# Score rows of 640 keys cut at key 384, and the second halves of the keys loaded from there

## The chip, the cores and the metric

The kernel runs on one core of a Trainium2 chip. The metric is the device time of one execution in microseconds (us). Three runs of the kernel before took 960.04, 960.36 and 960.93 us, so the median is 960.36 us.

## The reference

One layer of a hybrid decoder on 1024 positions of width 1024: a norm and one wide projection, then differential softmax attention (8 heads, two maps each) beside gated linear attention (4 heads), then an output projection and a norm around the residual. The change is in the differential attention. Per head `h`, query block of 128 rows and map `m`:

```python
s = jnp.einsum('bqhmd,bkhmd->bhmqk', qb, k)          # two maps of 64 dims
mask = key_pos[None, :] <= q_pos[:, None]            # causal
p = jax.nn.softmax(jnp.where(mask, s, -jnp.inf), axis=-1)
w = p[:, :, 0] - lam * p[:, :, 1]
out = jnp.einsum('bhqk,bkhv->bqhv', w, v)
```

Everything is computed to float32 accuracy. Each operand is kept as a rounded part `hi` and a remainder `lo`. For the scores the two parts of a map (64 dims each) lie one above the other in 128 partitions: `k` holds (hi, lo), `ks` holds (lo, hi), and two matmuls with the same query tile, `sc<-k,q` and `sc<-ks,q`, give the whole product.

## The kernel before, in words

The program has three stages. The first makes the projections by a fast block scheme (matmuls `x`, `y`, `z`) with the gated attention in between. The second, from about 615 us to 910 us of the profile, runs three streams that `merge` (L1238) lays into one program order by planned times: `all_scores` (L1376), `all_values` (L1480: transposes `wtr`, products `po`, norms `ms`) and `out_early` (L1585: parts of the output projection, `ypart`). The third finishes the output (`yps`). On PE, TensorE's queue, this order is kept as written. On the other engines and on SP, the queue of most loads, a scheduler that simulates a time line may reorder what does not depend on one another.

`all_scores` goes through the heads 0 to 7 and in each through the query blocks 7 down to 0. Block `qb` needs `n = (qb + 1) * 128` keys. `parts_of` (L1270) cuts `n` at 512, since a bank of PSUM holds 512 columns: n = 1024, 896, 768 and 640 make two parts, the smaller ones one. `scores` (L1299) runs one pair of matmuls a part into one of three banks in turn; DVE (VectorE) then adds the mask, stores the part in `p0` or `p1` and takes the row's minimum on the way (L1335; `maskt` is a strip of zeros with the triangle of one block at its end). ACT (ScalarE) makes the exponentials when a row's last part is in, POOL (GpSimd) and DVE weigh and subtract the maps.

Keys and queries lie in DRAM (`qk_d`) and are loaded in two halves of 512 keys by `load_qk` (L1151) through SP: one DMA a map for `q` and `k`, two for `ks`. A tile has a place named by its tag and pool: the second halves of all heads share `k1` and `ks1` in `kp`, the queries `q0` and `q1`; the first halves of even heads are in `k0`, `ks0` of `kp`, those of odd heads in `k0`, `ks0` of `smp`, the pool of stage two. A load into a place waits until PE has read the last tile there. The loads of head h + 1 are written behind query block 4 of head h (L1382 on), together with the second half of head 0's values `v` while h is 0.

`attn_norm` (L1431) of the last head keeps its gate in the places `q1` (first half) and `k1` (second half), which are free by then.

Of the kernel before, what the change touches and what calls it, by code (L numbers as in the profile page):

```python
# [8 lines left out]
F32 = mybir.dt.float32  # L9
F32R = mybir.dt.float32r  # L10
# [4 lines left out]
P = 128  # L15
S = 1024
# [15 lines left out]
def hymba_kernel(  # L32
# [47 lines left out]
    def cols(half):  # L80
        return slice(half * 512, half * 512 + 512)
# [14 lines left out]
    eps_t, mhalf = eps_t[:, :1], eps_t[:, 1:]  # L96
    pool.memset(eps_t, EPS)
    pool.memset(mhalf, -0.5)
    NZ = 512
    maskt = const.tile([P, NZ + P], F32, name="maskt")  # L100
    pool.memset(maskt, 0.0)
    pool.affine_select(
# [40 lines left out]
    def mm(*a, **k):  # L143
        tc.keep_in_program_order(pe.matmul(*a, **k))  # L144
# [32 lines left out]
    kp = ctx.enter_context(tc.tile_pool(name="kp", bufs=1))  # L177
# [969 lines left out]
    def chain(*streams):  # L1147
        for st in streams:
            yield from st

    def load_qk(h, n, half, maps=(0, 1)):  # L1151

        if maps[0]:
            t = qk[h, n, half]
        elif h % 2 and half == 0 and n != "q":
            t = smps[0].tile([P, 2, 512], F32R, tag=f"{n}0", name=f"{n}0")
        else:
            t = kp.tile([P, 2, 512], F32R, tag=f"{n}{half}", name=f"{n}{half}")
        for m in maps:
            d = qk_d["q" if n == "q" else "k"][h][m, :, :, cols(half)]  # L1160
            if n != "ks":
                ins = sp.dma_start(fp(t[:, m]), d.rearrange("t p s -> (t p) s"))
            else:
                for i in range(2):
                    ins = sp.dma_start(fp(t[64 * i : 64 * i + 64, m]), d[1 - i])
        qk_load[:] = [ins.ins]
        qk[h, n, half] = t

    qk, smps, qk_load = {}, [], []
# [97 lines left out]
        if first:  # L1267
            tc.keep_in_program_order(ins)

    def parts_of(n):  # L1270
        return [(0, n)] if n <= 512 else [(0, 512), (512, n)]

    def load_v(h):
        v = [smp.tile([P, NT, P], F32R, tag="v", name=f"v{t}", bufs=4) for t in range(2)]
# [24 lines left out]
    def scores(h, qb):  # L1299

        n = (qb + 1) * P
        qc = slice(qb % 4 * P, qb % 4 * P + P)
        st = const.tile([P, 6], F32, tag="stt", name="stt", bufs=4)
        if h == 0 and qb == NT - 1:
            for row, i in ((4, 7), (5, 6)):
                p1s[row] = pp.tile([P, (i + 1) * P], F32, tag=f"p0_{i}", name="p1", bufs=2)
        p0 = pp.tile([P, n], F32, tag=f"p0_{qb}", name="p0", bufs=1 + (qb > 5))
        if h == 0 and qb < 2:
            p1s[qb] = smp.tile([P, 512], F32, tag=("r", "fold")[qb], name="p1", bufs=1)
        p1 = p1s.pop(qb, None) or smp.tile([P, S], F32, tag="p1", name="p1", bufs=2)  # L1310
        for m, p in enumerate((p0, p1)):
            q = qk[h, "q", qb // 4][:, m, qc]
            parts = parts_of(n)
            if h == DA_HEADS - 1 and (qb, m) in ((1, 1), (0, 0), (0, 1)):

                parts = [(0, 512)]
            for i, (a, b) in enumerate(parts):
                sc = sc_bank("sc", [P, 512])
                for j, name in enumerate(("k", "ks")):
                    for half in range(2):  # L1320
                        lo, hi = max(a, half * 512), min(b, half * 512 + 512)
                        if lo < hi:
                            mm(
                                sc[:, lo - a : hi - a], q,
                                qk[h, name, half][:, m, lo - half * 512 : hi - half * 512],
                                start=(j == 0), stop=(j == 1),
                            )
                e = min(b, n)
                last = i == len(parts) - 1

                forced = (h, qb) == (0, NT - 2) or (h, qb, m) == (0, 3, 0)
                forced = forced or ((h, qb) == (0, 4) and m + i > 0)
                behind = tc.issue_after(lowest[0]) if forced else nullcontext()
                with behind:
                    ins = dve.tensor_tensor_reduce(  # L1335
                        p[:, a:e], sc[:, : e - a],
                        maskt[:, NZ + P - (e - a) :] if last else maskt[:, : e - a],
                        1.0, 3e38 if i == 0 else st[:, 4 + m : 5 + m], ALU.add, ALU.min,
                        st[:, m : m + 1] if last else st[:, 4 + m : 5 + m],
                    )  # L1340
                if (h, qb) == (0, NT - 1):
                    lowest[:] = [ins.ins]
                c = 0.08 + (e - a) / 512 * 0.56
                if last:
                    act.activation(
                        p[:, :n], p[:, :n], AF.Exp, bias=st[:, m : m + 1], scale=-1.0,
                        accum_out=st[:, 2 + m : 3 + m],
                    )
                if last and m:
                    rec = dve.reciprocal(st[:, 4:6], st[:, 2:4])  # L1350
                    if h == 0 and qb in (4, 5):
                        lowest[:] = [rec.ins]
                    pool.tensor_scalar(
                        p1[:, :n], p1[:, :n], st[:, 5:6], lam, ALU.mult, ALU.mult
                    )
                    if qb != 5:
                        while mixed:
                            with tc.issue_after(ins.ins):
                                mixed.pop(0)()

                    def mix_maps():
                        dve.scalar_tensor_tensor(
                            p0[:, :n], p0[:, :n], st[:, 4:5], p1[:, :n], ALU.mult, ALU.subtract
                        )
                        w[h, qb] = p0

                    if h == 0 and qb > 2:
                        mixed.append(mix_maps)
                    else:
                        mix_maps()  # L1370
                    c += 0.25 + n / 1024 * 1.4
                yield c
# [39 lines left out]
        dve.tensor_tensor(lo[:, :n], pt[:, :n], fp(hi[:, :n]), ALU.subtract)  # L1412
        return hi, lo

    turned_last, squared_last = [], []

    def weigh(po, half, kts, v, wt):

# [12 lines left out]
    def attn_norm(h, half, o, po):  # L1431
        if h == DA_HEADS - 1 and not half:
            with tc.issue_after(squared_last[1]):
                act.copy(o, po)
        if h < DA_HEADS - 1:
            gate = smp.tile([P, 512], F32, tag="gate", name="gate", bufs=2)
        else:
            gate = kp.tile([P, 512], F32, tag=("q1", "k1")[half], name="gate")
        with tc.issue_after(qk_load[0]):
            sp.dma_start(gate, g_d[h][:, cols(half)])  # L1440
        sq = smp.tile([P, 512], F32, tag="r", name="sq", bufs=1)


        hl = smp.tile([P, 512], F32R, tag="sq_hl", name="sq_hl", bufs=1)
        fold = smp.tile([P, 512], F32, tag="fold", name="fold", bufs=1)
        act.activation(fold[:64], o[64:], AF.Square)
        ending = h == DA_HEADS - 1 and half
        with tc.issue_after(turned_last[0]) if ending else nullcontext():
            act.activation(sq[:64], o[:64], AF.Square)
        dve.tensor_tensor(sq[:64], sq[:64], fold[:64], ALU.add)  # L1450
        ins = act.copy(hl[:64], sq[:64]).ins
        if ending:
            squared_last.append(ins)
        dve.tensor_tensor(hl[64:], sq[:64], fp(hl[:64]), ALU.subtract)
        if h == DA_HEADS - 1:

            dve.scalar_tensor_tensor(gate, o, sub_g, gate, ALU.mult, ALU.mult)
        for _ in range(4):
            yield 0.0
        n_tr[0] += 1  # L1460
        ms = bank(TR[n_tr[0] % 2], [P, 512], "ms")
        mm(ms, ones, hl, start=True, stop=True)
        if h == DA_HEADS - 1 and not half:
            opened[TR[n_tr[0] % 2]] = None
        r = smp.tile([P, 512], F32, tag="r", name="r", bufs=1)
        act.activation(r, ms, AF.Ln, bias=eps_t, scale=1.0 / P)
        ins = act.activation(r, r, AF.Exp, scale=-0.5).ins
        if ending:
            squared_last.append(ins)
        if h < DA_HEADS - 1:  # L1470
            dve.scalar_tensor_tensor(r, o, sub_g, r, ALU.mult, ALU.mult)
            pool.tensor_tensor(gate, r, gate, ALU.mult)
            sp.dma_start(mixd[h * P : (h + 1) * P, cols(half)], gate)
            stored.append(h)
        else:
            dve.tensor_tensor(gate, gate, r, ALU.mult)
            last_mix[half] = gate
        yield 0.0
# [231 lines left out]
    def last_times(st, dh, part, e):  # L1710
# [8 lines left out]
    T = 8 * 36.0  # L1719
    LAG, SOON = 34.0, 2.0  # L1720
    s_cost = sum(
        2 * sum(0.08 + (min(b, n) - a) / 512 * 0.56 for a, b in parts_of(n)) + 0.25 + n / 1024 * 1.4
        for n in range(P, S + 1, P)
    )
    merge(
# [121 lines left out]
```

## Time and profile before

| what | value |
|---|---|
| median of three runs | 960.36 us |
| the profiled execution | 960.34 us |
| its span, first to last instruction | 958.6 us |
| granted clock of TensorE, mean | 0.998 |
| bytes moved | 220.34 MB |
| loads of keys: `k` 32 of 256 KB, `ks` 64 of 128 KB | 5.5 us and 6.2 us to landing, median |

How to read the lines of the profile: PE is TensorE's matmuls, PEld its weight loads, L144 is the one line through which all matmuls go, so that they are told apart by the names `out<-in` and by shape. A line of a timeline begins with the start in us from the begin of the span and the duration in us. Matmuls are pipelined: the next one starts before the modelled end of the last, so the distance between starts is what one costs. Instructions that only issue a DMA are listed as SPq.

### The profile page before, as it was taken

To read this page: it belongs to the slowest core of one execution; us is meant where nothing else is said; L and a number is where in the kernel's file an instruction comes from. 1 tells how busy PE (TensorE), PEld (TensorE's weight loads), DVE (VectorE), ACT (ScalarE), POOL (GpSimd) and SP (SyncE) were. 2 spreads that over 40 slices of the span, in tenths; PEclk is the share of its full clock that TensorE was granted. 3 is DMA by queue.
4 is the path that set the end of the run, shared out by engine and by line. 5 is a ranking of instruction groups with operands and counts; after the bars stand their busy time and mean duration, and the time that the engine had idled before them with its cause. 6 is when DMAs were issued, how large, how long until landed. Compare 5 with 4: busy or idle time off the path is not lost.

```text
span 958.6 us, 14358 instructions
## 1 busy us (share of the span) xinstructions
PE 948.2 (99%) x4624; PEld 793.2 (83%) x4624; DVE 742.3 (77%) x1476; ACT 604.7 (63%) x1162; POOL 193.9 (20%) x263
## 2 busy tenths in 40 slices
PE   9999999999999999999999999999999999999997
PEld 7877788888888888888888888888888888888885
DVE  5998799996778787687767476588888888898464
ACT  7753355845777556577765444366677677787773
POOL 2001002222141112131100002122222222433321
PEclk9999999999999999999999999999999999999999
DMA  8546367487577897986755498996665679994776
GB/s 285 162 149 172 91 203 244 168 293 249 188 255 242 275 305 255 295 258 216 263 175 154 143 298 265 411 291 217 220 223 193 222 230 349 331 291 105 160 206 141
DMA packets 153258, 220.34 MB, mean 230 GB/s; under 512 B 15776, under 2 KB 85664, under 8 KB 153088
## 3 DMA queue, kind: packets, MB, share of 16 engines
q1 hardware_dynamic: 138736, 177.65, 57.8%
q0 software_dynamic: 14448, 41.79, 14.8%
q8 instruction: 36, 0.59, 0.3%
q14 instruction: 38, 0.31, 0.1%
HBM read 133.93 MB, written 88.60 MB: 232 GB/s over the span
## 4 chain that ended last, share of the span: by engine, by line
PE 96%; DVE 1%; ACT 1%; DMA 1%; issue 0%; POOL 0%; SPq 0%; DVEq 0%; ACTq 0%
PE x L144 23%; PE z L144 16%; PE y L144 16%; PE ypart L144 14%; PE sc L144 7%; PE po L144 5%; PE yps L144 4%; PE wtr L147 3%; PE gpo L144 3%; PE kv L144 1%; PE gkl_ps L144 1%; PE pa L144 1%; PE xT L147 1%; DMA x<-in_x_dram 1%; PE ms L144 0%; PE pk L147 0%
## 5 line engine op out<-in xcount | busy, mean ns | idle before, releaser
L66 ACT CAST w<-w_raw 128x512 fp32r<-128x512 f32 x138 | 85.1, 620 | 70.0 <-PE y L144 31.7
L66 ACT ACTIVATE p<-p,stt 128x896 f32<-128x896 f32 (+7 forms) x128 | 99.3, 777 | 30.8 <-DVE stt L66 29.9
L66 DVE TENSOR_TENSOR w<-w_raw,w 128x512 fp32r<-128x512 f32 x138 | 94.0, 684 | 31.5 <-ACT w L66 31.4
L66 ACT COPY s<-x 128x512 f32<-128x512 f32 x78 | 44.7, 584 | 65.1 <-PE x L144 64.9
L66 DVE CUSTOM_DVE_ANT_0 p<-sc,maskt 128x512 f32<-128x512 f32 (+3 forms) x128 | 74.2, 585 | 14.5 <-PE sc L144 13.2
L66 POOL TENSOR_SCALAR p<-p,stt,lam 128x1024 f32<-128x1024 f32 (+3 forms) x64 | 55.9, 874 | 143.9 <-DVE stt L66 143.8
L144 PE MATMUL z<-s_hi,w 128*128 128x512 f32 x320 | 80.1, 393 | 0.0
L144 PE MATMUL x<-s_hi,w 128*128 128x512 f32 x320 | 80.0, 392 | 0.0
L144 PE MATMUL y<-h_hi,w 128*128 128x512 f32 x320 | 80.0, 392 | 0.0
L144 PE MATMUL ypart<-wo_hi,m_hi 128*128 128x512 f32 x192 | 79.5, 414 | 0.1
L144 PE MATMUL ypart<-wo_hi,m_lo 128*128 128x512 f32 x192 | 75.5, 393 | 0.0
L144 PE MATMUL ypart<-wo_lo,m_hi 128*128 128x512 f32 x192 | 75.4, 393 | 0.0
L66 POOL DMA_DIRECT2D wo_d<-wo_hi x32 | 17.4, 543 | 270.4 <-ACT wo_hi L66 270.4
L144 PEld LDWEIGHTS z<-s_hi,w 128*128 128x128 f32 x320 | 59.8, 188 | 12.3
L144 PEld LDWEIGHTS x<-s_hi,w 128*128 128x128 f32 x320 | 59.7, 188 | 12.3
L144 PEld LDWEIGHTS y<-h_hi,w 128*128 128x128 f32 x320 | 59.7, 188 | 12.2
L144 PE MATMUL sc<-k,q 128*128 128x512 f32 (+1 forms) x192 | 68.9, 362 | 0.1
L144 PE MATMUL sc<-ks,q 128*128 128x512 f32 (+1 forms) x192 | 66.1, 347 | 0.0
L66 ACT CAST wt_hi<-wtr 128x512 fp32r<-128x512 f32 (+1 forms) x80 | 42.8, 534 | 29.0 <-PE wtr L147 28.3
L66 DVE TENSOR_TENSOR wt_lo<-wtr,wt_hi 128x512 fp32r<-128x512 f32 (+1 forms) x80 | 50.6, 633 | 9.9 <-ACT wt_hi L66 9.1
L66 DVE TENSOR_TENSOR w_raw<-w_raw 128x512 f32<-128x512 f32 x80 | 56.2, 703 | 1.4 <-DMA w_raw<-in_w_in_dram 0.4
L66 DVE TENSOR_TENSOR c<-z,s 128x512 f32<-128x512 f32 x48 | 32.8, 687 | 31.3 <-ACT s L66 19.3
(234 smaller groups left out, 2348.0 us busy)
## 6 DMA issues: line engine op xcount, KB each, us to landing
w_raw<-in_w_in_dram SPq DMA_DIRECT2D x40, 512.0 KB, 4.9
wo_d<-wo_hi POOLq DMA_DIRECT2D x32, 256.0 KB, 3.0
q<-q_d SPq DMA_DIRECT2D x32, 256.0 KB, 5.3
k<-k_d SPq DMA_DIRECT2D x32, 256.0 KB, 5.5
ks<-k_d SPq DMA_DIRECT2D x64, 128.0 KB, 6.2
wo_raw<-in_w_out_dram POOLq DMA_DIRECT2D x31, 256.0 KB, 5.0
v<-v_d SPq DMA_DIRECT2D x14, 512.0 KB, 7.7
wo_d<-gqd POOLq DMA_DIRECT2D x22, 256.0 KB, 4.1
```

The source lines that it names most:

```text
L66: ins = op(*a, **k)
L144: tc.keep_in_program_order(pe.matmul(*a, **k))
L147: tc.keep_in_program_order(pe.transpose(dst, src, ident))
```

## The change

From head 1 on a row of 640 keys is cut into 384 and 256 columns instead of 512 and 128. So that no part crosses a border of tiles, the second halves of keys of these heads are loaded from key 384 (`FROM`): tiles of 640 columns, of which rows of 768 keys and more use the part from key 512 on. These wider tiles have one place each in `smp` (`k1`, `ks1`); the first halves of odd heads move into the `k1`, `ks1` of `kp`, which only head 0's second halves had before, and those of even heads stay. The strip of zeros in the mask becomes 384 wide, and the first part of a wide row reads one zero column broadcast. The last head's two gates go into one tile in `q1`.

```diff
-    NZ = 512
+    NZ = 384
...
+    FROM = 384
+
     def load_qk(h, n, half, maps=(0, 1)):
 
         if maps[0]:
             t = qk[h, n, half]
-        elif h % 2 and half == 0 and n != "q":
-            t = smps[0].tile([P, 2, 512], F32R, tag=f"{n}0", name=f"{n}0")
+        elif h and half and n != "q":
+            t = smps[0].tile([P, 2, S - FROM], F32R, tag=f"{n}1", name=f"{n}1")
         else:
-            t = kp.tile([P, 2, 512], F32R, tag=f"{n}{half}", name=f"{n}{half}")
+            other = int(half == 0 and n != "q" and h % 2)
+            t = kp.tile([P, 2, 512], F32R, tag=f"{n}{half + other}", name=f"{n}{half}")
         for m in maps:
-            d = qk_d["q" if n == "q" else "k"][h][m, :, :, cols(half)]
+            cs = slice(FROM, S) if h and half and n != "q" else cols(half)
+            d = qk_d["q" if n == "q" else "k"][h][m, :, :, cs]
...
-    def parts_of(n):
-        return [(0, n)] if n <= 512 else [(0, 512), (512, n)]
+    def parts_of(n, h):
+        if n <= 512:
+            return [(0, n)]
+        cut = FROM if h and n == FROM + 2 * P else 512
+        return [(0, cut), (cut, n)]
...
-                    for half in range(2):
-                        lo, hi = max(a, half * 512), min(b, half * 512 + 512)
-                        if lo < hi:
-                            mm(
-                                sc[:, lo - a : hi - a], q,
-                                qk[h, name, half][:, m, lo - half * 512 : hi - half * 512],
-                                start=(j == 0), stop=(j == 1),
-                            )
+                    at = a if b <= 512 else a - (FROM if h else 512)
+                    mm(
+                        sc[:, : b - a], q, qk[h, name, int(b > 512)][:, m, at : at + b - a],
+                        start=(j == 0), stop=(j == 1),
+                    )
...
-                        maskt[:, NZ + P - (e - a) :] if last else maskt[:, : e - a],
+                        maskt[:, NZ + P - (e - a) :] if last else maskt[:, :1].to_broadcast([P, e - a]),
...
-            gate = kp.tile([P, 512], F32, tag=("q1", "k1")[half], name="gate")
+            if not ends:
+                ends.append(kp.tile([P, 2, 512], F32, tag="q1", name="gate"))
+            gate = ends[0][:, half]
```

The first place is SP's queue while head 0's scores run, where the loads of head 1 are issued. `k0_5984` and `ks0_5986` are head 1's first halves of keys, `k1_5979` and `ks1_5981` its second halves, `q1_5977` its queries 512 to 1023, `v0_5831` and `v1_5832` the values of head 0. Each key and query appears once for each of the two maps. Before:

```order
L1281 DMA v1_5832<-v0_d_112 128x512
L1162 DMA k0_5984<-k1_d_105 128x512
L1165 DMA ks0_5986<-k1_d_105 64x512 x2
L1162 DMA k0_5984<-k1_d_105 128x512
L1165 DMA ks0_5986<-k1_d_105 64x512 x2
L1162 DMA k1_5979<-k1_d_105 128x512
L1162 DMA q1_5977<-q1_d_97 128x512
L1165 DMA ks1_5981<-k1_d_105 64x512 x2
L1162 DMA q1_5977<-q1_d_97 128x512
L1162 DMA k1_5979<-k1_d_105 128x512
L1165 DMA ks1_5981<-k1_d_105 64x512 x2
L1391 DMA v0_5831<-v0_d_112 128x512
```

The same place of the changed kernel:

```order
L1288 DMA v1_5832<-v0_d_112 128x512
L1166 DMA k1_5979<-k1_d_105 128x640
L1169 DMA ks1_5981<-k1_d_105 64x640 x2
L1166 DMA k1_5979<-k1_d_105 128x640
L1169 DMA ks1_5981<-k1_d_105 64x640 x2
L1395 DMA v0_5831<-v0_d_112 128x512
L1395 DMA v1_5832<-v0_d_112 128x512
L1166 DMA k0_5984<-k1_d_105 128x512
L1166 DMA q1_5977<-q1_d_97 128x512
L1169 DMA ks0_5986<-k1_d_105 64x512 x2
L1166 DMA q1_5977<-q1_d_97 128x512
L1166 DMA k0_5984<-k1_d_105 128x512
```

The second halves went from behind the first halves to ahead of them, the second half of head 0's values from the end to the middle, and the first halves and the queries are last. PE's first score matmuls of head 1 read `k0_5984`, `q1_5977` and `ks0_5986` of the first map.

The second place is PE's queue at the 640 row of head 3 (query block 4), from the second part of its first map on. `k_6803` and `ks_6806` are first halves, `k_6795` and `ks_6798` second halves. Before:

```order
L144 MATMUL sc<-k_6795,q_6792 128x128
L144 MATMUL sc<-ks_6798,q_6792 128x128
L144 MATMUL ypart<-wo_hi,m_hi 128x512
L144 MATMUL ypart<-wo_hi,m_lo 128x512
L144 MATMUL ypart<-wo_lo,m_hi 128x512
L144 MATMUL sc<-k_6803,q_6792 128x512
L144 MATMUL sc<-ks_6806,q_6792 128x512
L147 MATMUL wtr<-ident,p_6894 128x128
L147 MATMUL wtr<-ident,p_6860 128x128
L147 MATMUL wtr<-ident,p_6823 128x128
L144 MATMUL sc<-k_6795,q_6792 128x128
L144 MATMUL sc<-ks_6798,q_6792 128x128
```

The same rows of the changed kernel:

```order
L144 MATMUL sc<-k_6795,q_6792 128x256
L144 MATMUL sc<-ks_6798,q_6792 128x256
L144 MATMUL ypart<-wo_hi,m_hi 128x512
L144 MATMUL ypart<-wo_hi,m_lo 128x512
L144 MATMUL ypart<-wo_lo,m_hi 128x512
L144 MATMUL sc<-k_6803,q_6792 128x384
L144 MATMUL sc<-ks_6806,q_6792 128x384
L144 MATMUL sc<-k_6795,q_6792 128x256
L144 MATMUL sc<-ks_6798,q_6792 128x256
L147 MATMUL wtr<-ident,p_6894 128x128
L147 MATMUL wtr<-ident,p_6860 128x128
L147 MATMUL wtr<-ident,p_6823 128x128
```

The second part of the second map moved from behind the three transposes to ahead of them; the widths are 384 and 256 instead of 512 and 128.

More of the change, by code (lines that the diff above doesn't have):

```diff
@@ L1312, in scores @@
             q = qk[h, "q", qb // 4][:, m, qc]
-            parts = parts_of(n)
+            parts = parts_of(n, h)
             if h == DA_HEADS - 1 and (qb, m) in ((1, 1), (0, 0), (0, 1)):
@@ L1413, in turn @@
         return hi, lo
-    turned_last, squared_last = [], []
+    turned_last, squared_last, ends = [], [], []
     def weigh(po, half, kts, v, wt):
@@ L1721, in hymba_kernel @@
     s_cost = sum(
-        2 * sum(0.08 + (min(b, n) - a) / 512 * 0.56 for a, b in parts_of(n)) + 0.25 + n / 1024 * 1.4
+        2 * sum(0.08 + (min(b, n) - a) / 512 * 0.56 for a, b in parts_of(n, 1)) + 0.25 + n / 1024 * 1.4
         for n in range(P, S + 1, P)
```

## The prediction

> **What bounds the kernel now.** I read the page first (busy time, then the chain that ended last), then the table of PE's waits.
>
> ```profile
> span 958.6 us, 14358 instructions
> PE 948.2 (99%) x4624; PEld 793.2 (83%) x4624; DVE 742.3 (77%) x1476; ACT 604.7 (63%) x1162; POOL 193.9 (20%) x263
> PE 96%; DVE 1%; ACT 1%; DMA 1%; issue 0%; POOL 0%; SPq 0%; DVEq 0%; ACTq 0%
> ```
>
> PE is busy for 99% of the span and makes 96% of the chain, so every tenth of a microsecond taken from PE's stream, or put into it as a wait, shows in the time. The table of waits has three rows for PE, 3.0 us together, all before the scores:
>
> ```profile
> PE spin L144 <- POOL idle L66: 1.5, 1, 1.5
> PE x L144 <- DVE w L66: 0.8, 1, 0.8
> PE xT L147 <- DVE x L66: 0.7, 1, 0.7
> ```
>
> PE takes its instructions in program order. A key that arrives late therefore stops everything behind it, the projections that stand between the scores too.
>
> **The shorter score matmuls.** The cost of a matmul is the distance from its start to the next start, not its own duration, since they are pipelined. From PE's timeline, head 3 (columns: start us, duration us):
>
> ```profile
> 717.12 0.33 PE L144 MATMUL sc<-k,q 128*128 128x384 f32 x1
> 717.29 0.34 PE L144 MATMUL sc<-ks,q 128*128 128x384 f32 x1
> 717.47 0.40 PE L144 MATMUL sc<-k,q 128*128 128x512 f32 x1
> ...
> 717.93 0.39 PE L144 MATMUL ms<-sq_hl,ones 128*128 128x512 f32 x1
> ...
> 723.78 0.28 PE L144 MATMUL sc<-k,q 128*128 128x256 f32 x1
> 723.90 0.28 PE L144 MATMUL sc<-ks,q 128*128 128x256 f32 x1
> 724.02 0.40 PE L144 MATMUL sc<-k,q 128*128 128x512 f32 x1
> ...
> 728.93 0.22 PE L144 MATMUL sc<-k,q 128*128 128x128 f32 x1
> 728.99 0.28 PE L144 MATMUL sc<-ks,q 128*128 128x128 f32 x1
> 729.10 0.45 PE L144 MATMUL ypart<-wo_hi,m_hi 128*128 128x512 f32 x1
> 729.38 0.40 PE L144 MATMUL ypart<-wo_hi,m_lo 128*128 128x512 f32 x1
> ```
>
> A pair (k, then ks) of 384 columns takes 717.47 - 717.12 = 0.35 us, a pair of 512 takes 717.93 - 717.47 = 0.46, a pair of 256 takes 724.02 - 723.78 = 0.24. The pair of 128 takes only 729.10 - 728.93 = 0.17, but the 512-wide matmul behind it takes 0.28 (729.10 to 729.38) where it takes 0.23 elsewhere, 0.05 more. So a map's row of 640 costs 0.46 + 0.17 + 0.05 = 0.68 us now and 0.35 + 0.24 = 0.59 then: 0.09 less. Seven heads (1 to 7) with one such row of two maps make 14, so **1.26 us less on PE**, all of it on the path. In the second map the transposes (three, 128 wide) now stand behind the 256-wide pair instead of ahead of the 128-wide one; the step after a short matmul is then paid behind the transposes. I cost that at nothing and take 1.26; at worst half of it goes (0.63).
>
> DVE's share does not change. From its groups by shape (mean ns behind the bar):
>
> ```profile
> L66 DVE CUSTOM_DVE_ANT_0 p<-sc,maskt 128x512 f32<-128x512 f32 x80 | 54.8, 685 | 13.1 <-PE sc L144 12.5
> ...
> L66 DVE CUSTOM_DVE_ANT_0 p<-sc,maskt,stt 128x512 f32<-128x512 f32 x16 | 11.9, 744 | 2.2 <-PE sc L144 2.1
> ...
> L66 DVE CUSTOM_DVE_ANT_0 p<-sc,maskt 128x384 f32<-128x384 f32 x16 | 8.5, 550 | 0.1
> L66 DVE CUSTOM_DVE_ANT_0 p<-sc,maskt,stt 128x256 f32<-128x256 f32 x16 | 7.4, 480 | 0.5
> L66 DVE CUSTOM_DVE_ANT_0 p<-sc,maskt,stt 128x128 f32<-128x128 f32 x16 | 5.5, 347 | 1.1 <-PE sc L144 0.6
> ```
>
> 685 + 347 = 1032 ns before, 550 + 480 = 1030 after. The first part of a wide row now adds one zero read again and again in place of a row of zeros. No row here has that operand. I bound each at -0.14 us (685 to 550, a shape less) and +0.06 us (685 to the 744 of the same shape with one operand more), and take 0: shape and number of streams stay.
>
> What hides DVE from PE is that the scores have three banks. Where DVE runs late that cover is thin, as in head 5:
>
> ```profile
> 799.88 0.68 DVE L66 CUSTOM_DVE_ANT_0 p<-sc,maskt 128x512 f32<-128x512 f32 x1
> ```
>
> The first part of its 640 row is read out from 799.88 to 800.56. The fourth part writes the bank of the first, and now comes sooner, ahead of the transposes. I put 0.1 us on it, 0 to 0.3.
>
> **The loads of head 1.** Here lies the larger term. SP's order of issue (shown with the change) turns round: before, head 1's first halves of keys went out first; now its second halves, 2.5 KB a row, and the rest of head 0's values go first, and the first halves and the queries come last, because their place is the one that head 0's second halves held. SP's timeline of before, and the landing times that the view of a single tile gives for the first key transfer, the query and the last pair of ks:
>
> ```profile
> 627.33 0.36 SPq L1162 DMA_DIRECT2D k<-k_d  x1
> ...
> 631.37 0.38 SPq L1162 DMA_DIRECT2D q<-q_d  x1
> ...
> L1162 SPq DMA_DIRECT2D k<-k_d x1: 364/364/364, 627.3 to 627.3; - x1
> DMA to landing us min/median/max: 4.5/4.5/4.5
> ...
> L1162 SPq DMA_DIRECT2D q<-q_d x1: 376/376/376, 631.4 to 631.4; - x1
> DMA to landing us min/median/max: 6.3/6.3/6.3
> ...
> L1165 SPq DMA_DIRECT2D ks<-k_d x2: 450/522/594, 635.4 to 635.9; - x2
> DMA to landing us min/median/max: 5.7/5.7/5.8
> ...
> 637.80 0.48 PE L144 MATMUL sc<-k,q 128*128 128x512 f32 x1
> 638.11 0.40 PE L144 MATMUL sc<-ks,q 128*128 128x512 f32 x1
> ...
> 641.07 0.39 PE L144 MATMUL sc<-ks,q 128*128 128x512 f32 x1
> ```
>
> The first key lands at 627.33 + 4.5 = 631.8, the query at 631.37 + 6.3 = 637.7, the last ks at 641.2 and 641.6. PE starts head 1 at 637.80: the query comes 0.1 us ahead of its use. **There is no slack here.** And the transfers are held up by the DMA engines, not by SP:
>
> ```profile
> 632.00:638.00 6.00, 6.00 (x39) 5.29 (x38) 5.93 (x24) 5.60 (x17) 2.07 (x3) 1.00 1.05 263
> 638.00:641.50 3.50, 3.50 (x18) 2.85 (x17) 3.45 (x8) 1.28 (x6) 1.23 (x3) 1.00 1.07 300
> 643.00:648.00 5.00, 5.00 (x26) 4.19 (x25) 3.11 (x10) 3.04 (x6) 1.21 (x1) 1.00 1.03 411
> ```
>
> (last columns: granted clock, DMA share, GB/s; the share is full in all three.) Now the sum. PE's first score pair of head 1 needs the first key half, the query and both ks pieces of map 0. Behind the first key transfer they now have: 64 KB more of that transfer, 960 KB of other second halves (4 x 160 + 320), 512 KB of values, then 256 + 256 + 256 KB of their own: 2304 KB. Before, the same 2304 KB lay between that landing and the last ks of head 1 (9 x 256 KB), so I read the time off directly: 641.4, the middle of 641.2 and 641.6. The ks matmul of map 0 stood at 638.11: **a wait of 3.3 us on PE**. Map 1 needs 768 KB more, 2.6 to 3.0 us at 300 or 263 GB/s, and PE asks for it 3.0 us later (641.07 - 638.11): no second wait. Ends: at 300 GB/s 2304 KB take 7.9 us, landing at 639.7, a wait of 1.6; at the pace of before between first key and query (1280 KB in 5.9 us) 10.6 us, landing at 642.4, a wait of 4.3.
>
> Later heads load with time in hand. The tightest is head 6: its ks were issued from 803.7 and landed after at most 8.5 us, the last at 807.9 + 5.3 = 813.2, for use from 815.78.
>
> ```profile
> L1165 SPq DMA_DIRECT2D ks<-k_d x4: 444/448/451, 803.7 to 807.9; - x4
> DMA to landing us min/median/max: 5.3/7.7/8.5
> ...
> 815.78 0.39 PE L144 MATMUL sc<-ks,q 128*128 128x512 f32 x1
> ```
>
> 256 KB more per head at the slow pace are 1.2 us: still in time. The last head's gate moves into a tile that comes free behind the same 640 row, and the mask's fill at the start gets shorter on POOL. Both at nothing: PE waits for neither in the table of waits.
>
> **Sum.** The profiled execution took 960.34 us (span 958.6), next to the median of 960.36. 960.34 - 1.26 + 3.3 + 0.1 = 962.48, I say **962.4**.
>
> **Rivals.**
> - The loads are faster than in that stretch, and the wait is hidden; this ends on the other side. At the 411 GB/s of 643 to 648 the 2304 KB take 5.7 us and land at 637.6, ahead of 638.11: 960.34 - 1.26 = 959.1. It decides below 6.3 us. For it: values, 512 KB of the sum, share no rows with the keys. Against: all windows of key loads lie at 263 to 300.
> - The shorter pairs bring nothing, because only the number of columns counts and 640 stay 640: 960.34 + 3.4 = 963.7. Against it: the rows of the 128-wide pair.
> - More waits: DVE's order shifts behind each 640 row, and banks come free late in several heads, 0.3 us in four of them: 963.6, or the loads at the slow end: 963.5.
>
> The Trainium skill ("TensorE: Matmul & The Clock Gate", section "Back-to-back issue gap") gives an isolated matmul N/2.4 + 2.5 ns, in which 512 + 128 and 384 + 256 are the same; by it the time is that of the second rival. The trace has 0.23 us for 512, near it, but 0.11 us for a 128-wide ks, about twice it. The Trainium skill ("DMA: Bandwidth & Descriptors", section "Bandwidth") states 341 GB/s for a 1 MB read; by it 2304 KB would be an estimated 6.9 us and the wait some 0.6 us, a time near the first rival's. The 263 GB/s above are short of it.
>
> **How the numbers follow.** Forecast (wait of 1.6 to 4.3, gain 0.6 to 1.26): 60%. Hidden loads: 13%. No gain: 10%. More waits: 12%. Something that makes it faster still, as an order on DVE that frees banks earlier: 5%. The forecast's own range is 960.7 to 964.0 (960.34 - 1.26 + 1.6, and 960.34 - 0.63 + 4.3). Leaving out the hidden loads and the 5%, the range is 960.2 to 964.2. A measurement tells 0.2% (1.9 us) from no change: slower begins at 962.3, close to my value, so the forecast splits into 33 (slower) and 27 (the same). Slower: 33 + 10 + 10 = 53%. The same: 27 + 13 + 2 and 1 of the last five, 43%. Faster: 4%.
>
> **What would show it.** PE's waits after: a row "sc" ended by DMA "ks" or "q" near 638, some 3 us. The steps of the 640 rows: 0.59 for two pairs. Later heads: no PE wait on DMA. It is wrong if head 1's first ks land before 638.5, or if waits on DVE appear behind the 640 rows.

## The result, and the profile after

| | runs | median us | lowest to highest us |
|---|---|---|---|
| kernel before | 6 | 960.94 | 960.04 to 961.23 |
| changed kernel | 6 | 968.26 | 964.49 to 970.09 |

The ratio is 1.0073, with a 95% interval of 1.0058 to 1.0087: 7.3 us slower. The direction was forecast, but the time lies above the range of 960.2 to 964.2. The six times of the changed kernel spread over 5.6 us, and the mean granted clock goes with them: 964.49 and 965.37 us at 0.998, 967.04 us at 0.995, 969.49, 969.54 and 970.09 us at 0.993 or 0.994.

The profiled execution took 969.49 us. First its page (span, busy time, chain), then its table of PE's waits:

```profile
span 967.8 us, 14353 instructions
PE 952.0 (98%) x4624; PEld 795.6 (82%) x4624; DVE 743.3 (77%) x1476; ACT 605.2 (63%) x1162; POOL 194.0 (20%) x263
PE 94%; DMA 2%; DVE 2%; ACT 1%; SPq 0%; issue 0%; POOL 0%; DVEq 0%; ACTq 0%
```

```profile
PE wtr L147 <- DVE p L66: 2.1, 1, 2.1
PE sc L144 <- DMA q<-q_d: 2.1, 1, 2.1
...
PE xT L147 <- DVE x L66: 1.2, 1, 1.2
...
PE sc L144 <- DMA ks<-k_d: 0.5, 1, 0.5
```

The span grew by 9.2 us, PE's busy time by 3.8. The two rows of `sc` on a DMA are the wait that was forecast. Two things were not: the wait of `wtr` for DVE, as long again, and the growth of the busy time although the matmuls were meant to be cheaper. PE's timeline at head 1 shows where the second comes from:

```profile
638.06 0.62 PE L147 MATMUL wtr<-ident,p 128*128 128x128 f32 x4
640.78 0.80 PE L144 MATMUL sc<-k,q 128*128 128x512 f32 x1 [2.10 <-DMA q<-q_d]
642.06 0.77 PE L144 MATMUL sc<-ks,q 128*128 128x512 f32 x1 [0.48 <-DMA ks<-k_d]
642.62 0.63 PE L144 MATMUL ypart<-wo_hi,m_hi 128*128 128x512 f32 x1
643.05 0.63 PE L144 MATMUL ypart<-wo_hi,m_lo 128*128 128x512 f32 x1
...
647.32 0.46 PE L144 MATMUL sc<-k,q 128*128 128x512 f32 x1
647.61 0.40 PE L144 MATMUL sc<-ks,q 128*128 128x512 f32 x1
```

The same place of the kernel before (the next two lines of it, 637.80 and 638.11, stand in the prediction):

```profile
637.42 0.62 PE L147 MATMUL wtr<-ident,p 128*128 128x128 f32 x4
```

From the transpositions `wtr` to the start of the ks matmul 0.69 us passed before (637.42 to 638.11) and 4.00 pass now (638.06 to 642.06): 3.3 us lost, 2.3 ahead of the query's matmul and 1.0 ahead of the ks. Losses by such starts are called losses by steps below. Then 512-wide matmuls follow each other at 0.43 us (643.05 - 642.62) instead of 0.23, until 647.3. The windows say why (the number ahead of the DMA share and the GB/s is the granted clock):

```profile
641.00:648.00 7.00, 6.52 (x17) 4.72 (x18) 2.53 (x7) 0.00 (x0) 0.45 (x1) 0.54 1.04 373
648.00:655.00 7.00, 7.00 (x37) 5.88 (x35) 4.92 (x13) 4.46 (x8) 1.21 (x1) 1.00 1.02 340
...
851.00:856.00 5.00, 4.95 (x21) 4.43 (x22) 2.43 (x7) 2.10 (x6) 1.30 (x2) 0.66 0.98 301
856.00:863.00 7.00, 7.00 (x41) 6.00 (x40) 6.03 (x20) 6.17 (x15) 2.87 (x4) 1.00 0.57 106
```

The granted clock is 0.54 behind the first stall and 0.66 behind the second, and 1.00 a few microseconds later. PE counts as busy there, so the table of waits shows none of it. Eleven steps of 0.43 at head 1 and a slow one at either edge cost 11 x 0.20 + 0.4 = 2.6 us; the slow steps at head 6, 852.1 to 855.6, cost 1.5.

The second stall is at head 6. Its 640 row (map 1) goes from ACT's exponential over DVE's reciprocal and POOL's multiplication to DVE's subtraction, for which the transposition `wtr` waits. Rows of the timeline of all engines there, in the changed kernel:

```profile
845.66 0.46 ACT L66 CAST wt_hi<-wtr 128x384 fp32r<-128x384 f32 x1
846.02 0.83 ACT L66 ACTIVATE p<-p,stt 128x640 f32<-128x640 f32 x1
...
847.67 0.15 DVE L66 RECIPROCAL stt<-stt 128x2 f32<-128x2 f32 x1
...
847.71 0.85 POOL L66 DMA_DIRECT2D y_d<-yst  x1 [4.89 <-ACT yst L66]
...
848.30 1.17 POOL L66 TENSOR_SCALAR p<-p,stt,lam 128x640 f32<-128x640 f32 x1
848.51 0.40 PE L144 MATMUL ypart<-wo_lo,m_hi 128*128 128x512 f32 x1
...
848.85 1.17 DVE L66 TENSOR_TENSOR sq_hl<-sq,sq_hl 64x512 fp32r<-64x512 f32 x1
...
850.13 0.87 DVE L66 SCALAR_TENSOR_TENSOR p<-p,stt,p 128x640 f32<-128x640 f32 x1
...
851.05 0.66 PE L147 MATMUL wtr<-ident,p 128*128 128x128 f32 x4 [2.14 <-DVE p L66]
```

The same links of the kernel before:

```profile
838.89 0.83 ACT L66 ACTIVATE p<-p,stt 128x640 f32<-128x640 f32 x1
...
839.85 0.17 DVE L66 RECIPROCAL stt<-stt 128x2 f32<-128x2 f32 x1 [0.67 <-ACT p L66]
840.12 0.87 POOL L66 TENSOR_SCALAR p<-p,stt,lam 128x640 f32<-128x640 f32 x1 [2.48 <-DVE stt L66]
841.75 0.87 DVE L66 SCALAR_TENSOR_TENSOR p<-p,stt,p 128x640 f32<-128x640 f32 x1
...
843.31 0.60 PE L147 MATMUL wtr<-ident,p 128*128 128x128 f32 x4
```

Before, 2.9 us pass from the exponential's end to the subtraction's end (839.72 to 842.62); after, 4.2 (846.85 to 851.00), and the exponential itself, which stood ahead of `fold` and `sq` on ACT, now stands behind both and a `wt_hi`. The scheduler, which orders each engine by planned times, exchanged them when the widths changed: `cut_512_again` below, with the loads of the changed kernel and the widths of before, has no wait at head 6. Each further link queues behind something too: the reciprocal behind the reading of row 3, POOL's multiplication behind the issue of a `y_d` transfer, the subtraction behind `sq_hl`.

So the 9.15 us of the profiled execution (969.49 - 960.34) read as: start 0.6 (`xT` waits 1.2 us, before 0.7; in the other profiles of this study that row is missing or 0.2 to 1.1), head 1's wait 3.3 and its slow steps 2.6, head 6's wait 2.3 and its slow steps 1.5, shorter pairs -1.3: together 9.0. What this reading doesn't show is whether the slow steps come from the idle time, and whether the two stalls are independent. That was tried.

### The profile page after: what moved, and what is told of

It reads as the page before. It is cut to its first block, busy times and chain, and to the rows that moved or that the text cites. A ratio compares the mean times of both kernels' runs of the same rounds, so it can differ in the third digit from the quotient of the medians.

```text
span 967.8 us, 14353 instructions
## 1 busy us (share of the span) xinstructions
PE 952.0 (98%) x4624; PEld 795.6 (82%) x4624; DVE 743.3 (77%) x1476; ACT 605.2 (63%) x1162; POOL 194.0 (20%) x263
## 4 chain that ended last, share of the span: by engine, by line
PE 94%; DMA 2%; DVE 2%; ACT 1%; SPq 0%; issue 0%; POOL 0%; DVEq 0%; ACTq 0%
PE x L144 23%; PE z L144 16%; PE y L144 16%; PE ypart L144 13%; PE sc L144 7%; PE po L144 5%; PE yps L144 4%; PE wtr L147 3%; PE gpo L144 3%; PE kv L144 1%; PE gkl_ps L144 1%; PE pa L144 1%; DMA x<-in_x_dram 1%; PE xT L147 1%; DMA ks<-k_d 1%; DMA k<-k_d 1%
## 5 line engine op out<-in xcount | busy, mean ns | idle before, releaser
L66 DVE CUSTOM_DVE_ANT_0 p<-sc,maskt 128x512 f32<-128x512 f32 (+3 forms) x128 | 72.2, 570 | 20.4 <-PE sc L144 19.7
L144 PE MATMUL sc<-k,q 128*128 128x512 f32 (+2 forms) x192 | 68.7, 362 | 2.2 <-DMA q<-q_d 2.1
L144 PE MATMUL sc<-ks,q 128*128 128x512 f32 (+2 forms) x192 | 66.0, 347 | 0.5 <-DMA ks<-k_d 0.5
```

The source lines that it names most:

```text
L66: ins = op(*a, **k)
```

## The experiments

All times are medians; "before" is the kernel before, run on the same chip in the same turn. Turns differ: "before" is 960.94 us beside the changed kernel and 960.26 to 960.91 below.

### Head 1's loads in map order

```diff
                     for maps in ((0, 1),) if h else ((0,), (1,)):
-                        for n in ("q", "k", "ks"):
-                            load_qk(h + 1, n, 1, maps)
-                        late = qk_load[0]
-                        for n in ("k", "ks"):
-                            load_qk(h + 1, n, 0, maps)
+                        with tc.issue_after(late) if maps == (1,) else nullcontext():
+                            for n in ("q", "k", "ks"):
+                                load_qk(h + 1, n, 1, maps)
+                            for n in ("k", "ks"):
+                                load_qk(h + 1, n, 0, maps)
+                        late = qk_load[0]
```

> Only SP's order of head 1's loads differs from the changed kernel: all five tiles of score map 0 first, then those of map 1, then the second half of head 0's values. Theory: the wait for q and ks at the start of head 1 (2.4 + 1.3 us in the profile) goes, and with it the stretch of doubled matmul steps behind it (0.43 us each instead of 0.23 for some 5 us, about 2.4 us); head 6's wait stays, so about 968.3 - 5.6 = 962.7 us, and the granted clock between 640 and 660 us is 1.00. Rival, wait alone: if the slow steps have another cause than the idle time, only 3.2 us go, 965.1. Rival, head 6 carries the loss: 967 or more.

Measured: 964.63 us (962.11 to 965.25, 7 runs; before 960.91), 3.6 less than the changed kernel, not 5.6. The clock is 1.00 behind head 1, as expected, but the wait didn't go: it moved to map 1, whose first halves now stood behind that map's 640-wide tiles. PE's timeline:

```profile
641.49 0.47 PE L144 MATMUL sc<-k,q 128*128 128x512 f32 x1 [0.78 <-DVE stt L66]
642.54 0.47 PE L144 MATMUL sc<-ks,q 128*128 128x512 f32 x1 [0.58 <-DMA ks<-k_d]
642.85 0.60 PE L147 MATMUL wtr<-ident,p 128*128 128x128 f32 x4
```

The first wait is put down to DVE, but DVE had been done for 0.2 us; the key transfer issued at 634.34 landed 7.1 us later, at 641.4, and is the real one. By steps 0.94 + 0.82 = 1.76 us are lost, and no slow steps follow. Head 6's wait and its slow stretch stayed (window 846 to 851 us: clock 0.66).

### Head 6's exponential ahead of fold

```diff
+        with tc.issue_after(lastexp[6, 4, 1]) if (h, half) == (5, 1) else nullcontext():
             act.activation(fold[:64], o[64:], AF.Square)
```

`lastexp` holds the exponential of each row and map.

> Only the order at head 6, row 4 differs from the changed kernel: ACT's fold of head 5's second half is issued behind the exponential of the 640-key row, which moves DVE's reciprocal and subtraction of that row ahead of the reading of row 3. Theory: the 2.1 us wait of wtr for DVE near 851 us goes, and the half-speed stretch behind it (about 1.6 us), while head 1's stall stays: about 968.3 - 3.7 = 964.6 us. Rival, the clock falls only behind the longer stall at head 1: 966.2. Rival, the wait moves to another instruction of the same row: 968.

Measured: 964.19 us (961.79 to 965.38, 7 runs; before 960.91), 4.1 less than the changed kernel. In the profile the wait of `wtr` near 847 us is down to 0.25 us, and the clock there is 1.00. Head 1's stall stays, though in this execution it is shorter (1.67 + 0.78 us by steps), with 0.43 us steps behind it until 644.5.

### Both repairs, and the cut back at 512 with the loads kept

Two kernels tell the cut from everything else. `both_repaired` holds both edits above. `cut_512_again` holds the first one and this:

```diff
-        cut = FROM if h and n == FROM + 2 * P else 512
-        return [(0, cut), (cut, n)]
+        return [(0, 512), (512, n)]
```

> The changed kernel with both repairs, so no long wait on TensorE and a clock of 1.00 throughout. Theory (waits, the clock behind them, and a gain of 1.26 us from the 384 + 256 columns): 959.0 to 959.8 us, faster than the kernel before by 1.2 us. Rival, shorter score matmuls gain nothing: 960.4 to 961. Rival, the 1.84 MB more of loads cost by themselves: 962 or more.

> Loads, places and the broadcast mask column of the changed kernel, with head 1's loads in the repaired order, but 640-key rows cut into 512 and 128 as before; TensorE, DVE, ACT and POOL have the order of the kernel before. Theory: as the kernel before, 960.4 to 961.0 us, and 1.26 us more than both_repaired. Rival, no gain from the cut: equal to both_repaired. Rival, the longer loads or the broadcast operand cost: 962 or more, with waits on q, k or DVE in the profile.

Measured: `both_repaired` 959.93 us (959.00 to 961.33, 11 runs), ratio to before 0.9992 (0.9984 to 1.0001); `cut_512_again` 961.30 us (960.21 to 961.80, 11 runs), ratio 1.0003 (0.9994 to 1.0012). Both are slightly above what was expected: a wait for ks at head 1 is left in their profiles, 0.39 and 0.73 us by steps. The wider loads, the places and the broadcast column together cost nothing that can be told from zero (0.4 us, though the 0.73 us is a wait for one of these loads). The medians differ by 1.37 us, with ranges that overlap. The profiled executions differ by 1.24 us (960.06 and 961.30); the wait for ks, 0.34 us shorter in `both_repaired`, is nearly balanced by 0.24 us that its `wtr` still waits at head 6, so about 1.2 us are the cut's. Where it gains, head 3, second map of the 640 row; first `both_repaired`, then `cut_512_again`:

```profile
730.18 0.33 PE L144 MATMUL sc<-k,q 128*128 128x384 f32 x1
730.35 0.34 PE L144 MATMUL sc<-ks,q 128*128 128x384 f32 x1
730.52 0.29 PE L144 MATMUL sc<-k,q 128*128 128x256 f32 x1
...
731.34 0.39 PE L144 MATMUL ypart<-wo_hi,m_lo 128*128 128x512 f32 x1
```

```profile
730.92 0.40 PE L144 MATMUL sc<-k,q 128*128 128x512 f32 x1
731.15 0.39 PE L144 MATMUL sc<-ks,q 128*128 128x512 f32 x1
...
731.62 0.31 PE L144 MATMUL sc<-k,q 128*128 128x128 f32 x1
...
732.16 0.40 PE L144 MATMUL ypart<-wo_hi,m_lo 128*128 128x512 f32 x1
```

From the row's first score matmul to the second projection behind it, with the three transposes inside: 1.16 us against 1.24, 0.08 less in the one map.

### The waits left in and filled

The changed kernel with matmuls that are thrown away in its two long waits; nothing waits less.

```diff
+                if (h, qb, m, i) == (1, NT - 1, 0, 0):
+                    for _ in range(12):
+                        mm(sc, qk[0, "q", 0][:, 0, :P], qk[0, "k", 0][:, 0], start=True, stop=True)
...
+        if (h, half, kts) == (6, 1, (0,)):
+            for _ in range(9):
+                mm(pt, qk[6, "q", 0][:, 0, :P], qk[6, "k", 0][:, 0], start=True, stop=True)
```

> The changed kernel with both of its long waits left in and filled with work on TensorE that is thrown away: 12 matmuls of 512 columns (2.8 us at 0.23) into the score bank ahead of head 1's first pair, and 9 (2.1 us) into the wtr bank ahead of head 6's first transposition; what they write is overwritten. Theory, the clock falls because TensorE idles: the time stays that of the waits alone, 964.3 to 965.4 us, the granted clock is 1.00 behind both, steps behind them are 0.23 us, and runs no longer spread from 964.5 to 970. Rival, the slow steps have another cause (transfers, the order itself): 968 to 970 and steps of 0.43 us stay, or the fill adds to the time.

Measured: 964.79 us (964.28 to 965.90, 5 runs; before 960.61), 3.5 us less than the changed kernel (3.1 when each is set against its own before) by doing more work, and the spread shrank from 5.6 us to 1.6. PE's timeline (the thirteenth of the first row is the real one), then the windows:

```profile
637.94 3.26 PE L144 MATMUL sc<-k,q 128*128 128x512 f32 x13
641.04 0.39 PE L144 MATMUL sc<-ks,q 128*128 128x512 f32 x1
641.26 0.39 PE L144 MATMUL ypart<-wo_hi,m_hi 128*128 128x512 f32 x1
641.49 0.39 PE L144 MATMUL ypart<-wo_hi,m_lo 128*128 128x512 f32 x1
```

```profile
641.00:648.00 7.00, 7.00 (x34) 5.78 (x34) 3.78 (x10) 2.92 (x5) 0.02 (x1) 1.00 1.05 340
...
851.00:856.00 5.00, 5.00 (x32) 4.33 (x31) 4.07 (x14) 4.98 (x15) 1.50 (x3) 1.00 0.89 234
```

The fill stands where the wait stood (the real ks starts at 641.04; in the changed kernel's profile at 642.06), but the steps behind it are 0.23 us and the clock is 1.00. At head 1 no wait is left behind the 12 matmuls, so how much shorter the bare wait would have been in this execution stays open. Loads and order are those of the changed kernel: the slow steps come from the idling, not from the transfers or the order.

### Loads by need, and the values alone

`loads_by_need` is `both_repaired` with map 1's loads in the order q, first halves, 640-wide second halves:

```diff
-                            for n in ("q", "k", "ks"):
+                            for n in ("q", "k", "ks") if maps[0] == 0 else ("q",):
                                 load_qk(h + 1, n, 1, maps)
...
+                        if maps == (1,):
+                            with tc.issue_after(qk_load[0]):
+                                for n in ("k", "ks"):
+                                    load_qk(h + 1, n, 1, maps)
```

> both_repaired with the loads of head 1's map 1 put in the order in which TensorE needs them: q and the first halves of the keys, then the 640-wide second halves, then head 0's values. Theory: the wait for ks left at head 1 in both_repaired (0.4 us in its profile, 0.7 in that of cut_512_again) goes, as 0.66 MB less stands ahead of it: 959.2 to 959.7 us, surely below the kernel before. Rival, the wait moves to the 640-wide second halves, needed 1.2 us later, or to the values: 959.9 to 960.6.

Measured: 959.50 us (959.12 to 961.11, 11 runs; before 960.61), ratio 0.9992 (0.9983 to 1.0000). PE waits for no DMA any more in the score stage of its profile.

`values_last` is `exp_first_h6` with the values issued last again:

```diff
-                        late = qk_load[0]
                         for n in ("k", "ks"):
                             load_qk(h + 1, n, 0, maps)
+                        late = qk_load[0]
```

> exp_first_h6 with one change of SP's order: the second half of head 0's values is issued behind head 1's key and q loads, as in the kernel before, while the 640-wide tiles of both maps still go ahead of q. It tells apart what of head 1's wait comes from the values (0.52 MB moved ahead) and what from the wider tiles. Theory: about 2.2 us of the 3.2 go with the values, so the wait is 0.5 to 1.5 us, too short for the clock to fall: 960.4 to 961.4 us. Rival, the order of the tiles alone makes the wait: 963 to 964, as exp_first_h6.

Measured: 961.37 us (959.39 to 963.86, 12 runs; before 960.61): of the 4.3 us between `exp_first_h6` and `both_repaired` 2.8 belong to the values (2.5 when each is set against its own before), slow steps included, and the rest to the wide tiles of map 1 ahead of q. That the median lies in the expected range is luck: the profiled execution (963.20 us) lost 1.36 + 0.79 us by steps, not 0.5 to 1.5, and the clock fell.

```profile
636.00:640.50 4.50, 2.76 (x18) 2.10 (x17) 3.21 (x10) 3.31 (x12) 1.37 (x3) 1.00 1.07 273
640.50:645.00 4.50, 4.50 (x14) 3.51 (x14) 2.53 (x7) 0.00 (x0) 0.45 (x1) 0.62 1.05 362
```

### Head 6: DVE's order alone, and the rest of the wait

`reciprocal_first` is `loads_by_need` without the edit on ACT; instead the reading of row 3 is issued behind row 4's reciprocal:

```diff
+                if (h, qb, m, i) == (6, 3, 1, 0):
+                    behind = tc.issue_after(recs[6, 4])
```

> loads_by_need without the change on ACT: ACT's order at head 6, row 4 is that of the changed kernel (fold and sq ahead of the exponential), and DVE's reciprocal of that row is pinned ahead of its reading of row 3; DVE's subtraction and POOL's multiplication then stand ahead of sq_hl and of a y_d transfer. It tells ACT's order apart from that of DVE and POOL, and gives a wait of a middle length. Theory: of the 2.3 us lost at head 6, about 1.4 go (0.6 of the reciprocal, 0.3 of POOL's issue of y_d, 0.6 of sq_hl), so TensorE waits 0.6 to 1.2 us there, too short for the clock to fall: 959.9 to 960.6 us and a granted clock of 1.00 between 840 and 870 us. Rival, ACT's order is what makes the wait: 2 us stay, with slow steps behind them, 962 to 963.

Measured: 960.76 us (959.93 to 961.84, 11 runs; before 960.26), 0.2 above the upper end, with a wait of middle length (0.93 us by steps) and no fall of the clock. The row of the table of waits, then the window:

```profile
PE wtr L147 <- DVE p L66: 0.8, 1, 0.8
```

```profile
840.00:870.00 30.00, 29.24 (x156) 24.70 (x155) 26.29 (x70) 24.04 (x54) 12.52 (x14) 1.00 0.92 255
```

So of the 2.3 us at head 6 the order behind the exponential made 1.4, and ACT's most of the rest (0.25 are left in `exp_first_h6`). `subtraction_first` is `loads_by_need` with the sum `sq<-sq,fold` issued behind the subtraction, `lastexp[6, 4]`:

```diff
+        with tc.issue_after(lastexp[6, 4]) if (h, half) == (5, 1) else nullcontext():
             dve.tensor_tensor(sq[:64], sq[:64], fold[:64], ALU.add)
```

> loads_by_need with DVE's sum of squares of head 5's second half issued behind the subtraction of head 6's row 4, which the transposition waits for (0.24 us in the profile of loads_by_need). Theory: that wait goes and nothing else moves: 959.0 to 959.6 us, about 0.25 us below loads_by_need, with an interval below the kernel before. Rival, the sum is late for what follows it, or DVE reaches the next row's reading later: 959.6 to 960.2.

Measured: 959.75 us (958.80 to 960.88, 11 runs; before 960.26), ratio 0.9996 (0.9987 to 1.0005). The last wait of 0.24 us is gone from the profile, but the time isn't lower than that of `loads_by_need`, whose runs stood beside a "before" 0.35 us higher. A quarter of a microsecond can't be told apart here, and whether this edit gains stays open.

## Why the prediction was wrong, point by point

- **PE bounds, and every wait shows: right.** It was even too weak, since a wait cost more than its length.
- **Shorter pairs, -1.26 us: right.** 1.37 by the two medians, about 1.2 by the two profiles, 0.08 in the one row read against 0.09 forecast. That row is one in which the transposes moved behind the short pair: their move cost at most 0.01 there, as taken. The rival "no gain", which the Trainium skill ("TensorE: Matmul & The Clock Gate", section "Back-to-back issue gap") gives by its formula, fell.
- **DVE neutral, the broadcast column at nothing: right.** `cut_512_again` carries that operand and stands at 1.0003 of before; its readings `p<-sc,maskt` of 512 columns, which have the operand in the first parts, take 686 ns on average against 685.
- **Head 1's loads, +3.3 us: right in cause and size** for the profiled execution, 3.3 us by steps, 2.3 of them put down to the query. The first ks was to land at 641.4 and landed at 641.9, in an execution that ran 0.6 us late from the start. That the size fits so well is partly luck, since it isn't the same in every execution: 2.5 us in the profile of `exp_first_h6`, which loads head 1 in the same order. The rival of hidden loads fell, and with it the wait of 0.6 us from the rate in the Trainium skill ("DMA: Bandwidth & Descriptors", section "Bandwidth").
- **The sum had no term for the clock: this step failed.** A wait was costed at its length. The two stalls were followed by slow steps that cost 2.6 and 1.5 us; filling both stalls took 3.5 us off the median.
- **Lateness on DVE, 0.1 us at head 5: this step failed too.** I looked for it at a score bank, where the first part of a row comes back sooner. It came at the other end of the row, between exponential and transposition, in head 6, where the scheduler exchanged rows on ACT, DVE and POOL: 2.3 us, all but 0.25 of it repaired by one edit of the order (`exp_first_h6`). The rival "more waits" had an order that shifts behind the 640 row, but named score banks that come free late, at 0.3 us in each of four heads. The prediction followed the order on SP and PE, not on ACT and POOL, where the row's chain lies too.
- **Together**: 962.4 forecast, plus the two clock terms and head 6's wait in place of 0.1, gives 962.4 + 4.1 + 2.2 = 968.7. These terms are those of the profiled execution, 969.49 us with a start 0.6 us late. The median was 968.26, and executions without slow steps lie lower.

## What to carry to other kernels

Where TensorE bounds a kernel, cost a new wait twice: its length, and the slow steps that can follow once it lasts some two microseconds; if it can't go, filling it with thrown-away matmuls already gets the second part back. When a change alters one size that a scheduler plans with, compare the order of every engine on the chain to the next TensorE instruction, not only the one edited. Repaired in both places, the change itself is worth little: `loads_by_need` stands 1.1 us below the kernel before, with an interval that reaches 1.0000, so a gain in total is likely and not shown.

## What the runs showed of the hardware

The granted clock falls to half behind a short stall, and it does so in whole windows of time. The trace records when it changes, and behind the first change of an execution the stretches between changes are multiples of 3.413 us: in the profile of the changed kernel full for 634.88 us (186 x 3.413), half for 6.83 (2 x), full for 204.80 (60 x), half for 3.41; in `loads_map0_first`, `exp_first_h6` and `values_last` one half stretch of 3.41 each, with steps of 0.427 us for 512 columns. Cut at these borders, the windows read as follows (behind the borders stand the length and PE's busy time; the third number from the end is the granted clock), first in the changed kernel, then in `loads_map0_first`:

```profile
637.16:640.57 3.41, 1.52 (x11) 1.15 (x9) 2.69 (x10) 2.77 (x11) 1.20 (x2) 1.00 1.07 322
640.57:643.99 3.42, 2.73 (x6) 1.86 (x7) 1.13 (x4) 0.00 (x0) 0.00 (x0) 0.50 1.06 340
...
848.79:852.20 3.41, 1.27 (x9) 1.11 (x9) 2.67 (x6) 1.62 (x5) 2.00 (x2) 1.00 1.07 287
852.20:855.61 3.41, 3.41 (x12) 2.93 (x11) 1.90 (x7) 1.44 (x5) 0.66 (x1) 0.50 1.02 310
```

```profile
638.36:641.77 3.41, 2.63 (x12) 1.76 (x10) 2.90 (x9) 0.57 (x3) 0.52 (x2) 1.00 1.05 241
641.77:645.18 3.41, 2.83 (x15) 2.26 (x15) 1.99 (x5) 1.64 (x3) 0.00 (x0) 1.00 1.05 409
```

The half clock begins at the end of a window in which PE lost much time by steps: 2.1 and 2.3 us in the changed kernel, 2.3 at head 6 of `loads_map0_first`, 2.2 in `exp_first_h6`, 2.1 in `values_last`. The second half window at head 1 of the changed kernel follows one that was at half clock itself and in which the 1.0 us for the ks were lost. Behind windows with 0.39 (`both_repaired`), 0.73 (`cut_512_again`) and 0.93 us (`reciprocal_first`) it stayed full. At head 1 of `loads_map0_first` the 1.76 us fell into two windows, 1.0 and 0.8, and the clock stayed full as well; the 2.1 us of `values_last`, two pieces too, lay in one. So in these profiles 1.0 us lost in one window at full clock left the clock alone and 2.1 halved it; where between them the limit lies, no run shows. The borders lie elsewhere in each execution (the first change comes 5.5 to 7.7 us into the span), so the same stall can fall into one window or be split. That fits the spread of the changed kernel: the mean clock of 0.998 at 964.49 and 965.37 us is that of the kernel before, the 0.993 of the profiled execution has three half windows in it, and an average over runs mixes such cases. It isn't shown, since no execution of the changed kernel at 0.998 was profiled.

The Trainium skill ("TensorE: Matmul & The Clock Gate", section "The HAM clock gate") gives a free-running window of about 3.4 us, half clock after an idle one, and N/1.2 ns for a matmul then, 426.7 ns for 512 columns. The step and the window agree, and the spread fits. That a whole window has to be idle does not: 2.1 us of 3.41, in two pieces, were enough here.
